# Loading, multiplying and splitting the first gate set of the v stage among the last units of the u stage

## The chip, the cores and the metric

The kernel runs on one core of one Trainium2 chip. The metric is the device time in microseconds (us) of one execution; of several runs the median is given. A separate execution was recorded by the hardware profiler, and its trace is what the rows further down come from.

## The reference, cut to what matters

The reference is a decoder trunk of two layers. Each layer has a mixer, a cross-attention to a memory, and an expert network (PEER); the change touches the expert network alone.

```
def peer_ffn(h, w_pq, sub_keys, expert_u, expert_v):
    q = (h @ w_pq).reshape(B, S, PEER_HEADS, 2, PEER_DQ // 2)
    scores = jnp.einsum('bshpd,hpkd->bshpk', q, sub_keys).astype(jnp.float32)
    top_s, top_i = lax.top_k(scores, K)
...
    best_s, best_pos = lax.top_k(cand_s, K)
    expert_idx = jnp.take_along_axis(cand_i, best_pos, axis=-1)
    gate = jax.nn.softmax(best_s, axis=-1).astype(h.dtype)
...
        u = jnp.take(expert_u, ic, axis=0)
        a = jnp.einsum('cd,chkd->chk', hc, u)
        w = gc * jax.nn.gelu(a, approximate=False)
        return jnp.einsum('chk,chkd->cd', w, jnp.take(expert_v, ic, axis=0))
```

`cand_s` holds the sums of the 16 x 16 pairs of the two halves' best scores. There are 8 heads, 16384 experts, 256 tokens and a model width of 1024. All numbers are float32.

## The kernel before

The kernel does not gather experts. It computes h times the whole of `expert_u` (the **u stage**), takes the Gelu of all of it, multiplies by a dense table of gates that is zero for the experts not chosen, and multiplies the product by the whole of `expert_v` (the **v stage**). Each stage runs over 128 **units**, here u0 to u127 and v0 to v127: a unit is 128 experts, that is one weight tile of 128 x 1024 (512 KB). Both layers run the same code, the second about 1050 us after the first.

**The stream.** All weight tiles of the kernel go through one `Stream` (L26 to L67). Its `load` starts a DMA from SyncE's queue (L49) into one of three `raw` buffers; its `prep` lets ScalarE round the tile to `hi` (L58) and VectorE take the rest `lo` (L60), each into one of three buffers. Before the matmuls of unit n are issued, `get` splits unit n+2 and then starts the load of unit n+5, which waits until the buffer of unit n+2 is split.

**A u unit** (`b_units`, L251 to L254) is 24 matmuls of 256 columns. After every second unit ScalarE and VectorE run `ev_u(i)` for the pair of units 2i and 2i+1: Gelu of the tokens 128 to 255 into `act` (L1005), Gelu of the tokens 0 to 127 into a buffer of the name `tt_` (L1007), which is stored to DRAM as `tdr[i]` while the gates of those tokens are not ready yet, and multiplied into the gate table `gt` (L1013) once they are. `pend` holds an `ev_u` back until the matmuls of the next unit are issued, or until `flush` is called.

**A v unit** (`v_mm`) is 12 matmuls of 512 columns (L1054), whose stationary operand is a split gate set. **Gate set w(n)** serves v(2n) and v(2n+1), and takes two steps. `w_load(n)` starts two DMAs on SyncE's queue into a `tt_` buffer: the gates of the tokens 128 to 255 from the table `gd` in DRAM (L1024), which GpSimd's indirect DMAs have summed up, and `tdr[n]` (L1029). `w_prep(n)` lets VectorE multiply the one half by `act` (L1038) and the other by `gt` (L1040), ScalarE round the set to `oh1` (L1041) and VectorE take the rest to `oh2` (L1042). There are two buffers of each name.

**The order.** Every engine runs its instructions in the order in which this Python code issues them (`manual_schedule`). After u127 the code issues `ev_u(63)`, then `w_load(0)`, `w_load(1)`, `w_prep(0)`, and then, ahead of v0, `w_load(2)` and `w_prep(1)`; ahead of each later even unit v(2n) stand `w_load(n+2)` and `w_prep(n+1)`.

Of the kernel before, what the change touches and what calls it, by code (L numbers as in the profile page):

```python
# [72 lines left out]
def paced(g, rate):  # L73

    credit = 0.0
    while True:
        credit += rate[0]
        while credit > 0:
            c = next(g, g)
            if c is g:  # L80
                return
            if c is None:
                break
            credit -= c
        yield
# [30 lines left out]
def build(tc, ctx, a):  # L116
# [28 lines left out]
    side = Side()  # L145
# [23 lines left out]
    hT = const.tile([128, KT, 512], F32R)  # L169
# [6 lines left out]
    def flush():  # L176
        while pend:
            pend.pop(0)()

    def unit(f):  # L180
        hi, lo = st.get()
        f(hi, lo)
        flush()
        side.tick()
# [55 lines left out]
    def b_units(src, n, evac, first=0):  # L240

        for i in range(first, first + n):
            if i % 2 == 0:
                ps = mm.tile([128, 2, 256], F32, name="mm")

            def f(hi, lo):
                h3 = hi.rearrange("p (k n) -> p k n", k=KT)
                l3 = lo.rearrange("p (k n) -> p k n", k=KT)
                o = ps[:, i % 2]
                for k in range(KT):  # L250
                    T.matmul(o, h3[:, k], src[:, k, 0:256], start=(k == 0), stop=False)  # L251
                    T.matmul(o, h3[:, k], src[:, k, 256:512], start=False, stop=False)  # L252
                for k in range(KT):
                    T.matmul(o, l3[:, k], src[:, k, 0:256], start=False, stop=(k == KT - 1))  # L254
            unit(f)
            if i % 2:
                pend.append(lambda i=i, ps=ps: evac(i // 2, ps))
# [92 lines left out]
    for l in range(L):  # L350
# [628 lines left out]
        direct = []  # L979

        def peer_task():
            for g in range(GROUPS):
                hs = range(HG * g, HG * g + HG)
                yield from keys_of(1, range(2 * hs.start, 2 * hs.stop))
                yield from scattered(hs)
            yield from keys_of(0, range(16))
            yield from select()
            c_top.close()
            gt[0] = pool(c_g1, "gp0").tile([128, 128, 128], F32, name="gt0")
            rate[0] = RATE[1]  # L990
            yield from g_build()
            yield None
            yield None
            direct.append(True)
        rate = [RATE[0]]
        t_p = side.add(paced(peer_task(), rate))
# [7 lines left out]
        def ev_u(i, ps):  # L1004
# [6 lines left out]
            direct.append(i)  # L1011
            g_ = gt[0][:, 2 * i:2 * i + 2]
            V.tensor_mul(g_, g_, t)  # L1013
        b_units(hT, 128, ev_u)
        assert not t_p in side.tasks
        flush()
        i_dir = direct[1]
        tw = {}

        def w_load(n):  # L1020
            if n < 64:
                tw[n] = t = pe.tile([128, 2, 256], F32, name="tt_")
                g_ = gd[l].rearrange("(n c p t) o -> n p c (t o)", c=2, p=128, t=128)
                i_ = nc.sync.dma_start(t[:, :, 128:256], g_[n]).ins  # L1024
                if n == 0:
                    for j_ in late:
                        tc.add_manual_dep(i_, j_.name, SYNC, reason="all gates")
                if n < i_dir:
                    nc.sync.dma_start(t[:, :, 0:128], tdr[n].rearrange("p (c t) -> p c t", c=2))  # L1029

        def w_prep(n):
            if n >= 64:
                return
            wh = pe.tile([128, 2, 256], F32R, name="oh1")
            wl = pe.tile([128, 2, 256], F32R, name="oh2")
            t = tw.pop(n)
            t0, t1 = t[:, :, 0:128], t[:, :, 128:256]
            V.tensor_mul(t1, t1, act[:, 2 * n:2 * n + 2])  # L1038
            if n < i_dir:
                V.tensor_mul(t0, t0, gt[0][:, 2 * n:2 * n + 2])  # L1040
                A.copy(wh, t)  # L1041
                V.tensor_sub(wl, t, wh.bitcast(F32))  # L1042
            else:
                for z, c_ in ((gt[0][:, 2 * n:2 * n + 2], slice(0, 128)), (t1, slice(128, 256))):
                    A.copy(wh[:, :, c_], z)
                    V.tensor_sub(wl[:, :, c_], z, wh[:, :, c_].bitcast(F32))
            tw[n] = (wh, wl)

        def v_mm(i, w, hi, lo, dds=(0, 1), tts=(0, 1)):
            for tt in tts:  # L1050
                h_, l_ = (z[:, i % 2, tt * 128:(tt + 1) * 128] for z in w)
                for st_, mv_, first in ((h_, hi, True), (l_, hi, False), (h_, lo, False)):
                    for dd in dds:
                        T.matmul(out[tt][dd], st_, mv_[:, dd * 512:(dd + 1) * 512],  # L1054
                                 start=(i == 0 and first), stop=(i == 127 and mv_ is lo))
        w_load(0)
        w_load(1)
        w_prep(0)
        c_ps.close()
        ops = pool(c_ps, "ops", space=PS)  # L1060
        out = [[ops.tile([128, 512], F32, name=f"out{tt}{dd}") for dd in range(2)] for tt in range(2)]
        for i in range(126):
            if i % 2 == 0:
                w_load(i // 2 + 2)
                w_prep(i // 2 + 1)
                w = tw.pop(i // 2)
            unit(lambda hi, lo: v_mm(i, w, hi, lo))
# [16 lines left out]
        for dd in range(2):  # L1084
            for tt in range(2):
                for c in range(2):
                    v_mm(126 + c, w, *last[c], (dd,), (tt,))
                if dd and not tt and l + 1 < L:
                    nx.turn(0, False)
                add_x(dd, tt, out[tt][dd])  # L1090
                if l + 1 == L:
                    xg[dd, tt] = new_t()
                    nx.squares(dd, (tt,))
                    V.tensor_mul(xg[dd, tt], x[:, tt, dd * 512:(dd + 1) * 512], gf[dd])
                    if dd:
                        nx.root(slice(tt, tt + 1))
# [92 lines left out]
```

## Time and profile before

| what | value |
|---|---|
| median of 3 runs | 2116.82 us (2116.72 to 2119.5) |
| the profiled execution: its own time | 2121.27 us |
| the profiled execution: its span | 2119.5 us |
| TensorE busy | 2089.5 us, 99% of the span |
| VectorE busy | 1496.0 us, 71% |
| ScalarE busy | 1125.5 us, 53% |
| mean granted TensorE clock | 0.996 |

The span runs from the first to the last instruction of the trace; what lies around it is 1.77 us. A row of the timeline gives the start, the length, the engine, the line and the number of instructions that it merges; behind it in brackets stands how long the engine had been idle, and what ended that. SPq is SyncE's DMA queue, PE is TensorE, DVE VectorE, ACT ScalarE.

### The profile page before, as it was taken

How to read it: one execution, taken by the hardware profiler on the slowest of the kernel's cores; microseconds unless marked ns; L12 is line 12 of the kernel's file. 1: busy time of each engine (PE TensorE's matmuls, PEld its weight loads, DVE VectorE, ACT ScalarE, POOL GpSimd, SP SyncE). 2: the span in 40 equal slices, each digit the busy share in tenths (PEclk: the TensorE clock that was granted, in tenths of full speed). 3: DMA queues.
4: the chain of work that ended last, by engine and by line, in shares of the span. 5: the costliest groups of instructions: out<-in, count | busy, mean ns of one | idle time of the engine just before them, and what ended most of it. 6: DMA issues, size and time to landing. Idle time of an engine off the chain costs nothing.

```text
span 2119.5 us, 35283 instructions
## 1 busy us (share of the span) xinstructions
PE 2089.5 (99%) x13508; PEld 1909.9 (90%) x13508; DVE 1496.0 (71%) x2593; ACT 1125.5 (53%) x1585; POOL 544.4 (26%) x565
## 2 busy tenths in 40 slices
PE   8999999999999999999999999999999999999998
PEld 7899899999999888888888998999999997888886
DVE  5775589988654577776676756999987446777766
ACT  5745556546654444444466455655566544444454
POOL 0120037787820000000012100478877100000000
PEclk9999999999999999999999999999999999999999
DMA  6664458887665677776667545588876656777765
GB/s 240 230 209 161 160 158 206 212 202 178 139 176 180 197 243 240 243 241 218 215 222 251 176 154 172 165 203 217 200 167 147 176 187 203 239 244 239 238 217 174
DMA packets 225609, 426.07 MB, mean 201 GB/s; under 512 B 54304, under 2 KB 134560, under 8 KB 224160
## 3 DMA queue, kind: packets, MB, share of 16 engines
q1 hardware_dynamic: 185696, 415.83, 61.7%
q0 software_dynamic: 36864, 0.15, 4.9%
q10 hardware_dynamic: 2880, 7.85, 1.1%
q8 instruction: 105, 1.72, 0.3%
q14 instruction: 64, 0.52, 0.1%
HBM read 410.50 MB, written 30.02 MB: 208 GB/s over the span
## 4 chain that ended last, share of the span: by engine, by line
PE 68%; issue 23%; POOL 5%; DMA 2%; ACT 1%; DVE 1%; POOLq 0%; SPq 0%; ACTq 0%
PE out L1054 16%; PE mm L252 11%; PE mm L251 11%; PE mm L254 11%; POOL gd L881 5%; PE mm L194 4%; PE mm L196 4%; PE mm L195 4%; PE gps L960 1%; PE sps L807 1%; DMA kt<-keys 1%; PE att L698 1%; PE att L729 1%; DMA gd<-gv,gi 1%; PE att L434 0%
## 5 line engine op out<-in xcount | busy, mean ns | idle before, releaser
L60 DVE TENSOR_TENSOR lo<-raw,hi 128x1024 fp32r<-128x1024 f32 x680 | 831.6, 1228 | 362.3 <-ACT hi L58 355.7
L58 ACT CAST hi<-raw 128x1024 fp32r<-128x1024 f32 x680 | 711.7, 1050 | 465.4 <-PE mm L252 263.1
L251 PE MATMUL mm<-hT,hi 128*128 128x256 f32 x2272 | 563.0, 285 | 0.0
L1054 PE MATMUL out<-hi,oh 128*128 128x512 f32 x2048 | 552.6, 391 | 9.0 <-ACT oh L1041 9.0
L252 PE MATMUL mm<-hT,hi 128*128 128x256 f32 x2272 | 557.1, 283 | 0.0
L881 POOL DMA_INDIRECT gd<-gv,gi x256 | 474.7, 1854 | 199.7 <-DVE tv L794 81.3
L1054 PEld LDWEIGHTS out<-hi,oh 128*128 128x128 f32 x2048 | 386.6, 189 | 90.0 <-ACT oh L1041 9.4
L251 PEld LDWEIGHTS mm<-hT,hi 128*128 128x128 f32 x2272 | 436.1, 192 | 0.3
L252 PEld LDWEIGHTS mm<-hT,hi 128*128 128x128 f32 x2272 | 435.7, 192 | 0.2
L254 PE MATMUL mm<-hT,lo 128*128 128x256 f32 x2272 | 318.8, 283 | 0.0
L1054 PE MATMUL out<-lo,oh 128*128 128x512 f32 x1024 | 317.8, 390 | 0.0
L260 POOL TENSOR_TENSOR rstd<-rstd,mhalf 128x2 f32<-128x2 f32 (+1 forms) x8 | 5.5, 688 | 1180.4 <-DVE rstd L300 1180.4
L254 PEld LDWEIGHTS mm<-hT,lo 128*128 128x128 f32 x2272 | 293.0, 192 | 0.0
L1054 PEld LDWEIGHTS out<-lo,oh 128*128 128x128 f32 x1024 | 193.1, 189 | 40.4
L889 POOL MEMSET mhalf<- 1x1 f32 x256 | 159.1, 622 | 0.0
L961 ACT ACTIVATE gt<-gps 128x512 f32<-128x512 f32 x64 | 68.9, 1114 | 40.4 <-PE gps L960 40.4
L966 DVE TENSOR_TENSOR oh<-slot 128x1024 f16<-128x1024 f16 x64 | 44.2, 690 | 51.3 <-PE gps L960 51.2
L960 PE MATMUL gps<-oh,oh 128*128 128x128 f16 x512 | 68.7, 296 | 0.4 <-issue 0.2
L194 PE MATMUL mm<-hi,hT 128*128 128x512 f32 x160 | 64.0, 400 | 0.0
L196 PE MATMUL mm<-lo,hT 128*128 128x512 f32 x160 | 62.6, 391 | 0.0
L195 PE MATMUL mm<-hi,hT 128*128 128x512 f32 x160 | 62.4, 390 | 0.0
L960 PEld LDWEIGHTS <-oh 128*128 128x128 f16 x512 | 53.9, 118 | 3.6 <-issue 0.8
(911 smaller groups left out, 2345.7 us busy)
## 6 DMA issues: line engine op xcount, KB each, us to landing
raw<-u SPq DMA_DIRECT2D x256, 512.0 KB
raw<-v SPq DMA_DIRECT2D x256, 512.0 KB
raw<-w_in_a SPq DMA_DIRECT2D x40, 512.0 KB
gd<-zeros SPq DMA_DIRECT2D x64, 256.0 KB
raw<-pq SPq DMA_DIRECT2D x32, 512.0 KB
raw<-w_in_b SPq DMA_DIRECT2D x16, 512.0 KB
raw<-wkv_b SPq DMA_DIRECT2D x16, 512.0 KB
raw<-w_out SPq DMA_DIRECT2D x16, 512.0 KB
```

The costliest lines, as they stand in the source:

```text
L58: self.nc.scalar.copy(hi, r)
L60: self.nc.vector.tensor_sub(lo, r, hi.bitcast(F32))
L194: T.matmul(ps[tt], sh, h3[:, kk], start=(k == 0), stop=False)
L195: T.matmul(ps[tt], sl, h3[:, kk], start=False, stop=False)
L196: T.matmul(ps[tt], sh, l3[:, kk], start=False, stop=(k == KT - 1))
L251: T.matmul(o, h3[:, k], src[:, k, 0:256], start=(k == 0), stop=False)
L252: T.matmul(o, h3[:, k], src[:, k, 256:512], start=False, stop=False)
L254: T.matmul(o, l3[:, k], src[:, k, 0:256], start=False, stop=(k == KT - 1))
L881: i_ = G.indirect_dma_start(gd[l], bass.IndirectOffsetOnAxis(ap=gi[:, h, c:c + 1], axis=0), gv[:, h, c:c + 1], None, compute_op=OP.add).ins
L889: G.memset(mhalf[0:1, 8:9], 0.0)
L960: T.matmul(ps[:, i], a0[:, 1, :, i], b0[:, w, :, i], start=(w == 0), stop=(w == 1))
L1054: T.matmul(out[tt][dd], st_, mv_[:, dd * 512:(dd + 1) * 512], start=(i == 0 and first), stop=(i == 127 and mv_ is lo))
```

## The change

`w_load(0)` is issued after u123 in place of after u127, and `w_prep(0)` after u125. For this `flush` is called after u123 too, so that `ev_u(61)` is issued ahead of the split of u126 in place of behind the matmuls of u124. `w_load(1)` stays behind `ev_u(63)`, and all that follows stays as it was. The definitions of `w_load`, `w_prep` and `v_mm` move up in the text, unchanged but that `i_dir` is now written `direct[1]`. No instruction is added or taken away. L1024, L1029, L1038, L1040, L1041, L1042 and L1054 of before are L1020, L1025, L1034, L1036, L1037, L1038 and L1050 of the changed kernel.

```
-        b_units(hT, 128, ev_u)
-        assert not t_p in side.tasks
-        flush()
-        i_dir = direct[1]
         tw = {}
...
-                if n < i_dir:
+                if n < direct[1]:
...
+        b_units(hT, 124, ev_u)
+        flush()
+        assert not t_p in side.tasks
         w_load(0)
+        b_units(hT, 2, ev_u, 124)
+        w_prep(0)
+        b_units(hT, 2, ev_u, 126)
+        flush()
         w_load(1)
-        w_prep(0)
         c_ps.close()
```

**SyncE's queue at the end of the u stage, layer 0.** The five tiles `raw` are those of v0 to v4; `tt__8435` is the buffer of w(0) before and `tt__8305` that of after, the next ones are w(1) and w(2). Before:

```order
L49 DMA raw_8275<-v 128x1024
L49 DMA raw_8306<-v 128x1024
L49 DMA raw_8340<-v 128x1024
L49 DMA raw_8371<-v 128x1024
L49 DMA raw_8405<-v 128x1024
L1024 DMA tt__8435<-gd0_94 128x2x128
L1029 DMA tt__8435<-tdr_96 128x2x128
L1024 DMA tt__8438<-gd0_94 128x2x128
L1029 DMA tt__8438<-tdr_96 128x2x128
L1024 DMA tt__8456<-gd0_94 128x2x128
```

After:

```order
L49 DMA raw_8275<-v 128x1024
L1020 DMA tt__8305<-gd0_94 128x2x128
L1025 DMA tt__8305<-tdr_96 128x2x128
L49 DMA raw_8313<-v 128x1024
L49 DMA raw_8343<-v 128x1024
L49 DMA raw_8380<-v 128x1024
L49 DMA raw_8414<-v 128x1024
L1020 DMA tt__8444<-gd0_94 128x2x128
L1025 DMA tt__8444<-tdr_96 128x2x128
L1020 DMA tt__8456<-gd0_94 128x2x128
```

The two loads of w(0) have moved from behind the tile of v4 to behind the tile of v0, and the loads of w(1) now stand where those of w(0) stood.

**ScalarE at the end of the u stage, layer 0.** The first `hi` of each list is that of u126, the next ones are u127, v0, v1 and v2; the pairs L1005 and L1007 are `ev_u(61)`, `ev_u(62)` and `ev_u(63)`. Before:

```order
L58 CAST hi_8302<-raw_8210 128x1024
L1005 ACTIVATE act_3204<-mm_8236 128x256
L1007 ACTIVATE tt__8333<-mm_8236 128x2x128
L58 CAST hi_8336<-raw_8241 128x1024
L58 CAST hi_8367<-raw_8275 128x1024
L1005 ACTIVATE act_3204<-mm_8301 128x256
L1007 ACTIVATE tt__8398<-mm_8301 128x2x128
L58 CAST hi_8401<-raw_8306 128x1024
L1005 ACTIVATE act_3204<-mm_8366 128x256
L1007 ACTIVATE tt__8432<-mm_8366 128x2x128
L1041 CAST oh1_8441<-tt__8435 128x512
L1041 CAST oh1_8459<-tt__8438 128x512
```

After:

```order
L1005 ACTIVATE act_3204<-mm_8236 128x256
L1007 ACTIVATE tt__8302<-mm_8236 128x2x128
L58 CAST hi_8309<-raw_8210 128x1024
L58 CAST hi_8339<-raw_8241 128x1024
L1037 CAST oh1_8369<-tt__8305 128x512
L58 CAST hi_8376<-raw_8275 128x1024
L1005 ACTIVATE act_3204<-mm_8308 128x256
L1007 ACTIVATE tt__8407<-mm_8308 128x2x128
L58 CAST hi_8410<-raw_8313 128x1024
L1005 ACTIVATE act_3204<-mm_8375 128x256
L1007 ACTIVATE tt__8441<-mm_8375 128x2x128
L1037 CAST oh1_8459<-tt__8444 128x512
```

The rounding of w(0) has moved from behind `ev_u(63)` to ahead of the split of v0, `ev_u(61)` has moved ahead of the split of u126, and the rounding of w(1) still stands behind `ev_u(63)` and ahead of the split of v2. VectorE's list moves in the same way. The order of TensorE's matmuls is unchanged.

## Rows read from the trace of the kernel before

**Rows 1.** Part 1 of the page: busy time of each engine.

```profile
PE 2089.5 (99%) x13508; PEld 1909.9 (90%) x13508; DVE 1496.0 (71%) x2593; ACT 1125.5 (53%) x1585; POOL 544.4 (26%) x565
```

**Rows 2.** Waits of TensorE: in total (us), times, longest; the two largest.

```profile
PE out L1054 <- ACT oh L1041: 9.0, 2, 4.8
PE mm L267 <- DMA cm<-c_main: 3.8, 1, 3.8
```

**Rows 3.** Timeline of TensorE, layer 0: end of u127, start of v0, v1.

```profile
705.14 1.12 PE L254 MATMUL mm<-hT,lo 128*128 128x256 f32 x8
...
711.02 2.07 PE L1054 MATMUL out<-hi,oh 128*128 128x512 f32 x4 [4.76 <-ACT oh L1041]
...
715.75 1.07 PE L1054 MATMUL out<-hi,oh 128*128 128x512 f32 x4
```

**Rows 4.** The same in layer 1; the last row is the 19th matmul.

```profile
1754.92 1.12 PE L254 MATMUL mm<-hT,lo 128*128 128x256 f32 x8
...
1760.27 2.07 PE L1054 MATMUL out<-hi,oh 128*128 128x512 f32 x4 [4.22 <-ACT oh L1041]
...
1767.33 1.08 PE L1054 MATMUL out<-hi,oh 128*128 128x512 f32 x4
```

**Rows 5.** Windows: length, busy time per engine, granted clock, DMA share, GB/s.

```profile
259.00:260.00 1.00, 0.27 (x3) 0.08 (x2) 0.10 (x1) 0.00 (x0) 0.00 (x0) 1.00 0.67 250
260.00:261.00 1.00, 0.99 (x8) 1.00 (x9) 0.00 (x0) 0.22 (x1) 0.00 (x0) 1.00 1.03 307
...
711.02:715.30 4.28, 4.28 (x10) 3.32 (x11) 3.26 (x5) 1.57 (x2) 0.00 (x0) 0.52 0.21 61
1760.27:1766.87 6.60, 6.60 (x17) 5.11 (x17) 4.07 (x6) 2.61 (x3) 0.00 (x0) 0.54 0.27 94
718.00:1048.00 330.00, 330.00 (x1457) 273.26 (x1456) 231.50 (x304) 161.18 (x200) 0.00 (x0) 1.00 0.76 234
```

**Rows 6.** Timeline of w(0) from its loads to its rounding, both layers.

```profile
705.42 0.39 SPq L1024 DMA_DIRECT2D tt__8435<-gd  x1
705.86 0.59 SPq L1029 DMA_DIRECT2D tt__8435<-tdr  x1
...
709.52 0.42 DVE L1038 TENSOR_TENSOR tt__8435<-tt__8435,act 128x256 f32<-128x256 f32 x1 [2.11 <-DMA tt__8435<-gd]
709.89 0.43 DVE L1040 TENSOR_TENSOR tt__8435<-tt__8435,gt 128x256 f32<-128x256 f32 x1
710.35 0.62 ACT L1041 CAST oh<-tt__8435 128x512 fp32r<-128x512 f32 x1 [3.40 <-DVE tt__8435 L1040]
...
1755.20 0.48 SPq L1024 DMA_DIRECT2D tt__19653<-gd  x1
...
1758.60 0.42 DVE L1038 TENSOR_TENSOR tt__19653<-tt__19653,act 128x256 f32<-128x256 f32 x1 [1.40 <-DMA tt__19653<-gd]
1759.14 0.42 DVE L1040 TENSOR_TENSOR tt__19653<-tt__19653,gt 128x256 f32<-128x256 f32 x1
1759.60 0.62 ACT L1041 CAST oh<-tt__19653 128x512 fp32r<-128x512 f32 x1 [2.86 <-DVE tt__19653 L1040]
```

**Rows 7.** Timeline, layer 0: tile loads, splits of u127, v0; w(1)'s rounding, split of v2.

```profile
693.27 11.85 SPq L49 DMA_DIRECT2D raw<-v  x5
...
697.78 1.23 DVE L60 TENSOR_TENSOR lo<-raw,hi 128x1024 fp32r<-128x1024 f32 x1 [1.32 <-ACT hi L58]
...
699.58 1.05 ACT L58 CAST hi<-raw 128x1024 fp32r<-128x1024 f32 x1 [1.83 <-PE mm L252]
...
712.40 0.62 ACT L1041 CAST oh<-tt__8438 128x512 fp32r<-128x512 f32 x1 [1.43 <-DVE tt__8438 L1040]
712.92 1.04 ACT L58 CAST hi<-raw 128x1024 fp32r<-128x1024 f32 x1
...
714.00 1.22 DVE L60 TENSOR_TENSOR lo<-raw,hi 128x1024 fp32r<-128x1024 f32 x1 [0.26 <-ACT hi L58]
```

**Rows 8.** Timeline of TensorE: a short wait earlier in layer 0.

```profile
260.01 0.68 PE L807 MATMUL sps<-kt,q 128*128 128x128 f32 x4 [0.75 <-DMA kt<-keys]
```

More of the change, by code (lines that the diff above doesn't have):

```diff
@@ L1038, in w_prep @@
             V.tensor_mul(t1, t1, act[:, 2 * n:2 * n + 2])
-            if n < i_dir:
+            if n < direct[1]:
                 V.tensor_mul(t0, t0, gt[0][:, 2 * n:2 * n + 2])
```

## The prediction

> **What bounds the kernel now.** I read the page's busy times first: TensorE is busy for 2089.5 of 2119.5 us [rows 1], so the time is TensorE's own work plus what little it stands idle, and 30 us is all that any reordering could touch. The waits of TensorE come next, to see where that idle time sits: the largest entry is 9.0 us in two waits, both of the first matmul of the v stage, for ScalarE's rounding of a gate set [rows 2]. That is one wait in each layer, at just the place that the change moves. The timeline of both places then says what one such wait costs, and here there is more than the idle time.
>
> Layer 0. The eight last matmuls of u127 start at 705.14, and eight of 0.28 us that fill 1.12 start 0.12 apart; so the next matmul would be due at 705.14 + 8 x 0.12 = 706.10. It starts at 711.02 [rows 3]: 4.92 us lost. In the long middle of the v stage 1457 matmuls take 330 us, 0.2265 each, at a granted clock of 1.00 [rows 5]. The 13th matmul of the stage would so be due 12 x 0.2265 = 2.72 after the first, at 713.74, and starts at 715.75 [rows 3]: another 2.01 us lost, in a stretch in which the granted clock was 0.52, that is the lower of the two levels (1.2 GHz) nearly throughout [rows 5]. Before the clock fell, TensorE had done nothing but wait.
>
> Layer 1 reads the same: due at 1754.92 + 0.96 = 1755.88, started at 1760.27, 4.39 lost; the 19th matmul due 18 x 0.2265 = 4.08 later at 1764.35, started at 1767.33 [rows 4], 2.98 lost at a granted clock of 0.54 [rows 5].
>
> The two places cost 4.92 + 2.01 + 4.39 + 2.98 = **14.30 us**. Of this 9.31 is waiting and 4.99 is the clock.
>
> **Why TensorE waits there.** SyncE starts the loads of w(0) at 705.42, when the u stage is all but over; the first multiplication starts 4.10 later, the rounding 0.83 after that at 710.35, and TensorE 0.67 after that [rows 6, 3]. In layer 1 the load takes 3.40 [rows 6]. Nothing in this chain needs the end of the u stage; it is only issued there.
>
> **The change, part by part.**
>
> *The loads of w(0)* now stand behind the tile load of v0, which starts at 693.27 [rows 7], so they start at about 693.7 (the gates themselves were summed long before). By the two loads of before they are there 3.4 to 4.1 later, by 697.8. Queued behind them on SyncE are the tile loads of v1 to v4; each of these waits for a split that comes later anyway, the first at some 697, and the two loads hold SyncE for 0.39 + 0.59 us [rows 6]. Cost nothing.
>
> *The early flush* puts `ev_u(61)` ahead of the split of u126 on ScalarE and VectorE. That split comes some 1.6 us later by the length of what is now ahead of it; u126 starts on TensorE at 706.10 - 2 x 2.88 = 700.34, over 2 us after the split is done. Cost nothing, and u127's split waits for TensorE as before.
>
> *The multiplications and the split of w(0)* follow VectorE's part of u127, which runs from 697.78 for 1.23 [rows 7]. So they start at 699.0, and with the steps of before (0.37, 0.46, and a rounding of 0.62 [rows 6]) the rounding runs from 699.85 to 700.45. Queued behind it on ScalarE is the rounding of v0's tile, which ran at 699.58 [rows 7] and now starts at some 700.4; with 1.08 until VectorE starts on its part and 1.22 for that (712.92, 714.00 [rows 7]) v0 is split at 702.7. TensorE needs it at 706.10: a cover of 3.4 us. If the load of w(0) came late, the first 1.2 us (697.8 to 699.0) and then these 3.4 would have to go before TensorE waits. So v0 starts at 706.10 and 1755.88, all 9.31 us of waiting go, and as nothing is left that idles TensorE, the 4.99 of the clock go too.
>
> *What is late next: w(1).* Its loads take exactly the place on SyncE that those of w(0) had, behind the tile of v4, and its rounding stands ahead of v2's split on ScalarE. So I take w(1) at the times that w(0) had: rounding at 710.35, v2's rounding 0.52 later (712.40 to 712.92 [rows 7]) from 710.87 to 711.92, VectorE's part from 711.95 to 713.17. But v2 is now due at 706.10 + 24 x 0.2265 = 711.54. It waits 0.38 for `hi`, and its fifth matmul, the first that uses `lo`, is due at 711.92 + 0.91 = 712.83 and waits another 0.34. In layer 1 the rounding at 1759.60 [rows 6] gives `hi` at 1761.17 against 1761.32, no wait, and `lo` at 1762.42 against 1762.23: 0.19. Together 0.38 + 0.34 + 0.19 = **0.91 us** given back. From both sides: nothing, if the loads of w(1) land some 0.7 earlier than those of w(0) did; or about 3 us a layer if they land 2.5 later. I take 0.91, since the loads before them in the queue are the same.
>
> The Trainium skill, DMA: Bandwidth & Descriptors, section Anatomy of one DMA, gives a DMA some 2.0 us and then its bytes at 436 GB/s; for 128 KB that is an estimate of 2.3 us. The rows here say 3.4 and 4.1, with other transfers under way, and the measurement decides; by the page v2 would not wait at all and the sum would be 14.3.
>
> *After v2.* Each later set has the same buffers and the same order as before. From 718 to 1048 TensorE never idled [rows 5], with VectorE busy for 231.5 of 330 us and ScalarE for 161.2, so the split has room to catch up; a set that is 0.4 late at v2 is not late again at v6.
>
> **The sum.** 14.30 - 0.91 = 13.39 us. Span: 2119.5 - 13.4 = 2106.1, and the profiled execution's own 2121.27 would be 2107.9. That execution was 4.45 us above the median of the runs; I take the same 13.4 off the median: 2116.82 - 13.4 = **2103.4 us**.
>
> **The rivals.**
>
> *The clock is not given back.* The new short waits at v2 could make the clock fall as the long ones did, or the timed runs could lose less to the clock than the profiled one. Then only 9.31 - 0.91 = 8.4 go: 2108.4. Against it: a wait of 0.75 us earlier in the layer [rows 8] left the granted clock at 1.00 in the windows around it [rows 5], and the waits that I expect are shorter. The Trainium skill, TensorE: Matmul & The Clock Gate, section A second HAM failure mode, tells of short idles between groups of matmuls that made the clock go back and forth; one or two waits do not repeat like that, and the trace speaks against it. Chance 0.08.
>
> *The wait moves to w(1) and grows (slower than before).* Before, a late w(1) was covered by the 7 us of layer 0's gap and slow clock; now nothing covers it. Each us that its loads land later is one us at v2, and a wait that long would bring the slow clock back at 2.0 to 3.0 a layer. A layer breaks even at a wait of about 7.15 - 2.5 = 4.65 us, a landing some 4 us later than rows 6 show, at 8 us in place of 4.1. At 12 us in both layers it would be 2 x (8.4 + 2.5) = 21.8 against 14.3 saved: 2124.3. For it: more data is now asked for in less time. Against it: the DMAs stood at a share of 0.76 at full pace [rows 5], and no load in rows 6 took over 4.1. Chance 0.05.
>
> *The change does nothing.* The order on SyncE, ScalarE and VectorE does move; but if the load of w(0) took over 10 us from 693.7, for instance behind the tile loads, TensorE would wait as before: 2116.8. Chance 0.04.
>
> **How the numbers follow.** About 0.2%, 4.2 us here, is what a measurement of this kernel can tell from no change. Forecast with its own bounds (up to 3 us more wait, up to 1 us less): 0.83, faster. Clock not given back: 0.08, faster. Slower rival: 0.05, of which all is slower. No change: 0.04. So faster 0.91, same 0.04, slower 0.05. Range: the low end has the clock cost 2.98 in both layers and no new wait, 2116.82 - (9.31 + 5.96) = 2101.5; the high end is the first rival's, 2108.4. Between them lies over 0.8.
>
> **What would show it.** In the profile of the changed kernel: no wait of TensorE before the first v matmul; a granted clock of 1.00 in the 5 us after it; the first gate multiplication near 699.0 and the next one near 709.5; a wait of TensorE of at most 0.4 us at v2, for `hi` or `lo`; a span near 2106. It would be wrong if the first v matmul still waits, if v2 waits for over 1 us, or if the clock falls in its first units.

## The result and the profile after

The changed kernel takes 2106.51 us (median of 4 runs, 2105.09 to 2109.22), the kernel before 2117.68 us (2116.72 to 2119.5). The ratio is 0.9948 with a 95% interval of 0.9931 to 0.9965: 11.2 us by the medians, 11.0 (7.4 to 14.6) by the ratio. The forecast was 13.4 us, a time of 2103.4. One timed execution of the kernel without the early flush (e5 below) ran at a mean granted clock of 0.851 and took 2259.15 us; it is left out of e5's median and ratio.

The profiled execution of the changed kernel has a span of 2107.4 us. The waits of TensorE answer to [rows 2]: in total, times, longest.

```profile
PE mm L267 <- DMA cm<-c_main: 4.0, 1, 4.0
PE mm L228 <- ACT hi L58: 1.9, 1, 1.9
PE att L434 <- issue: 1.5, 1, 1.5
PE out L1050 <- ACT hi L58: 1.2, 1, 1.2
```

The two waits for the rounding of w(0), 9.0 us, are gone. One wait of a v matmul is left, 1.2 us, and it is for the `hi` of a tile. The timeline of TensorE in layer 0, which answers to [rows 3], says which tile:

```profile
702.96 1.12 PE L254 MATMUL mm<-hT,lo 128*128 128x256 f32 x8
703.92 1.09 PE L1050 MATMUL out<-hi,oh 128*128 128x512 f32 x4
...
708.93 0.61 PE L1050 MATMUL out<-lo,oh 128*128 128x512 f32 x2
710.73 1.20 PE L1050 MATMUL out<-hi,oh 128*128 128x512 f32 x4 [1.18 <-ACT hi L58]
711.99 0.73 PE L1050 MATMUL out<-lo,oh 128*128 128x512 f32 x2
712.56 1.08 PE L1050 MATMUL out<-hi,oh 128*128 128x512 f32 x4
713.48 0.62 PE L1050 MATMUL out<-lo,oh 128*128 128x512 f32 x2
713.93 1.07 PE L1050 MATMUL out<-hi,oh 128*128 128x512 f32 x4
```

v0 is due at 702.96 + 8 x 0.12 = 703.92 and starts at 703.92. The 25th matmul, the first of v2, is due 24 x 0.2266 = 5.44 later at 709.36 and starts at 710.73: 1.37 lost. The 37th, the first of v3, is due at 712.08 and starts at 713.93: 1.85 lost by then. Of the further 0.48 us, 0.36 lie ahead of the first `lo` matmul of v2, which starts 1.26 behind the first of v2 where 0.91 is the usual distance, and 0.12 right behind it. In layer 1, which answers to [rows 4], the same reading gives:

```profile
1749.39 1.12 PE L254 MATMUL mm<-hT,lo 128*128 128x256 f32 x8
1750.36 1.09 PE L1050 MATMUL out<-hi,oh 128*128 128x512 f32 x4
...
1756.13 1.20 PE L1050 MATMUL out<-hi,oh 128*128 128x512 f32 x4
1757.39 0.74 PE L1050 MATMUL out<-lo,oh 128*128 128x512 f32 x2
...
1759.36 1.08 PE L1050 MATMUL out<-hi,oh 128*128 128x512 f32 x4
```

v0 starts at its due time; v2 is 0.34 late, v3 0.85, and 0.87 stays lost. The windows, columns as in [rows 5], show the clock around the wait at v2 in both layers:

```profile
706.00:711.00 5.00, 3.82 (x17) 2.89 (x16) 1.75 (x4) 1.89 (x3) 0.00 (x0) 1.00 0.26 78
711.00:712.00 1.00, 0.94 (x5) 0.41 (x4) 1.00 (x2) 0.62 (x1) 0.00 (x0) 1.00 0.00 0
...
1755.00:1760.00 5.00, 4.79 (x20) 3.31 (x19) 3.84 (x6) 2.79 (x5) 0.00 (x0) 1.00 0.31 103
```

The granted clock is 1.00 in all of them, through the wait of 1.18 us too. So the two places lose 1.85 + 0.87 = 2.72 us where they lost 14.30: 11.58 us gained at the places that the change touches, against 11.2 by the medians. The spans differ by 12.1. The other 0.5 us is the balance of two differences in stretches in which the change moves nothing: the u stage of layer 0 ended 2.18 earlier (703.92 against 706.10), and from v3 of layer 0 to v0 of layer 1 the execution took 1.73 longer; among the waits in between, that of L434 is the largest.

The rows of w(0) and w(1) answer to [rows 6]; here are those of layer 0, then the loads and first multiplication of w(1) in layer 1.

```profile
691.72 0.39 SPq L1020 DMA_DIRECT2D tt__8305<-gd  x1
...
703.04 0.43 SPq L1020 DMA_DIRECT2D tt__8444<-gd  x1
...
696.74 0.42 DVE L1034 TENSOR_TENSOR tt__8305<-tt__8305,act 128x256 f32<-128x256 f32 x1
...
708.31 0.43 DVE L1034 TENSOR_TENSOR tt__8444<-tt__8444,act 128x256 f32<-128x256 f32 x1 [3.08 <-DMA tt__8444<-gd]
...
709.11 0.62 ACT L1037 CAST oh<-tt__8444 128x512 fp32r<-128x512 f32 x1 [4.33 <-DVE tt__8444 L1036]
709.63 1.99 ACT L58 CAST hi<-raw 128x1024 fp32r<-128x1024 f32 x2
...
1749.47 1.42 SPq L1020 DMA_DIRECT2D tt__19662<-gd  x1
...
1753.46 0.43 DVE L1034 TENSOR_TENSOR tt__19662<-tt__19662,act 128x256 f32<-128x256 f32 x1 [1.79 <-DMA tt__19662<-gd]
```

w(0) is loaded 12.2 us ahead of v0's due time and multiplied 7.2 ahead of it, without a wait. w(1) is what TensorE now waits for, by way of v2's tile: its load takes 5.27 us from its issue to the first multiplication (3.99 in layer 1), the rounding follows 0.80 later, and v2's rounding is queued behind that.

### The profile page after: what moved, and what is told of

Read it like the earlier page. It is cut to its first block, busy times and chain, and to the rows that moved or that the text cites. A ratio compares the mean times of both kernels' runs of the same rounds, so it can differ in the third digit from the quotient of the medians.

```text
span 2107.4 us, 35289 instructions
## 1 busy us (share of the span) xinstructions
PE 2085.3 (99%) x13508; PEld 1906.2 (90%) x13508; DVE 1494.4 (71%) x2593; ACT 1124.7 (53%) x1585; POOL 541.0 (26%) x565
## 4 chain that ended last, share of the span: by engine, by line
PE 66%; issue 24%; POOL 5%; DMA 2%; DVE 2%; ACT 1%; SPq 0%; POOLq 0%; ACTq 0%; DVEq 0%
PE out L1050 16%; PE mm L252 11%; PE mm L251 11%; PE mm L254 11%; POOL gd L881 5%; PE mm L194 4%; PE mm L196 4%; PE mm L195 4%; PE gps L960 1%; PE sps L807 1%; PE att L698 1%; PE att L729 1%; DVE lo L60 1%; DMA gd<-gv,gi 1%; ACT hi L58 0%
## 5 line engine op out<-in xcount | busy, mean ns | idle before, releaser
L1050 PE MATMUL out<-hi,oh 128*128 128x512 f32 x2048 | 549.1, 389 | 1.3 <-ACT hi L58 1.2
L1050 PEld LDWEIGHTS out<-hi,oh 128*128 128x128 f32 x2048 | 384.1, 188 | 81.9 <-ACT hi L58 2.2
L1050 PE MATMUL out<-lo,oh 128*128 128x512 f32 x1024 | 316.7, 389 | 0.1
L1050 PEld LDWEIGHTS out<-lo,oh 128*128 128x128 f32 x1024 | 192.1, 188 | 40.6 <-DVE lo L60 1.0
```

## The experiments

For each kernel the table gives how late v0 starts and what is lost in all by v5 (the 61st matmul), worked out as above from the timeline of its profiled execution, and the time. Beside each median stands that of the kernel before, measured with it on the same chip.

| kernel | layer 0: v0, v5 | layer 1: v0, v5 | lost in both | median us (before) | ratio, 95% interval |
|---|---|---|---|---|---|
| before | 4.92, 6.93 | 4.39, 7.38 | 14.3 | | |
| changed | 0, 1.85 | 0, 0.87 | 2.7 | 2106.51 (2117.68) | 0.9948 (0.9931 to 0.9965) |
| changed, a1 | 0, 1.50 | 0, 0.61 | 2.1 | 2108.19 (2118.67) | 0.9954 (0.9941 to 0.9968) |
| changed, a2 | 0, 1.20 | 0, 0.53 | 1.7 | 2107.22 (2118.51) | 0.9944 (0.9930 to 0.9958) |
| e1, gap filled | 4.23, 4.64 | 4.37, 4.79 | 9.4 | 2114.41 (2118.67) | 0.9978 (0.9969 to 0.9988) |
| e2, loads alone | 2.68, 3.13 | 2.68, 4.66 | 7.8 | 2113.92 (2118.67) | 0.9978 (0.9967 to 0.9988) |
| e3, w(1) loaded early | 0, 0.03 | 0, 0.03 | 0.1 | 2105.11 (2118.67) | 0.9937 (0.9924 to 0.9951) |
| e4, v2 split first | 0, 0.03 | 0, 0.83 | 0.9 | 2106.04 (2118.35) | 0.9945 (0.9932 to 0.9959) |
| e5, no early flush | 0, 0.41 | 0, 0.62 | 1.0 | 2108.25 (2118.35) | 0.9957 (0.9942 to 0.9971) |
| e7, the same again | 0, 1.76 | 0, 0.79 | 2.6 | 2108.39 (2118.51) | 0.9949 (0.9935 to 0.9963) |
| e6, 1 MB ahead of w(1) | 0, 5.72 | 0, 6.54 | 12.3 | 2116.74 (2118.35) | 0.9994 (0.9984 to 1.0003) |
| e6, 2 MB ahead of w(1) | 0, 8.99 | 0, 8.58 | 17.6 | 2122.72 (2118.35) | 1.0029 (1.0018 to 1.0040) |

**The gap with TensorE at work.** Is the slow start of the v stage a price of the idle time, or would the first v matmuls be slow anyway? The kernel before, with filler:

```
         w_load(0)
         w_load(1)
         w_prep(0)
+        fill = mm.tile([128, 2, 256], F32, name="mm")
+        for k in range(32):
+            T.matmul(fill[:, 0], hT[:, k % KT, 0:128], hT[:, k % KT, 0:256], start=(k == 0), stop=(k == 31))
```

> The kernel before, with 32 matmuls of 256 columns into a spare accumulator issued between u127 and v0, so that TensorE works through most of the gap while w(0) is fetched and split as before. Their result is not used. They take 32 x 0.12 = 3.8 us of a gap of 4.2 to 4.8. Theory (a gap costs its idle time and then a stretch at the lower clock): v0 starts as late as before, 4.9 and 4.4 us behind its due time, but the granted clock stays at 1.00, the 13th matmul of layer 0 and the 19th of layer 1 come 2.0 and 3.0 us earlier against the first, and the time falls by 5.0 us. Rival (the first matmuls of the v stage are slow for another reason, such as new weights or accumulators): the clock or the spacing is as before, no change in time.

Measured: 4.3 us faster by the medians, 4.7 (2.5 to 6.6) by the ratio. The timeline of TensorE in layer 0, and two windows:

```profile
705.10 4.00 PE L1061 MATMUL mm<-hT 128*128 128x256 f32 x32
709.33 1.46 PE L1054 MATMUL out<-hi,oh 128*128 128x512 f32 x4 [0.22 <-ACT oh L1041]
710.62 0.62 PE L1054 MATMUL out<-lo,oh 128*128 128x512 f32 x2
...
712.46 1.07 PE L1054 MATMUL out<-hi,oh 128*128 128x512 f32 x4
...
705.00:709.30 4.30, 4.10 (x35) 3.90 (x33) 1.19 (x3) 1.28 (x3) 0.00 (x0) 1.00 0.72 231
709.30:714.00 4.70, 4.67 (x19) 3.58 (x20) 3.75 (x6) 2.60 (x3) 0.00 (x0) 1.00 0.19 56
```

v0 still starts 4.2 us late, for w(0), but the clock stays at 1.00 and the 13th matmul comes 3.13 after the first where it came 4.73 after it before [rows 3]. The timed executions say the same: all ten of this kernel have a mean granted clock of 0.999, the nineteen of the kernel before beside it 0.995 to 0.998. So the slow clock is the price of the idle gap. The price is a little less than the forecast said: 0.41 and 0.42 us are lost behind v0 even so, nearly all by its fifth matmul; two of the first four need the remainder of w(0) (`oh2`), which VectorE starts on only as v0 starts. At the slow clock that wait was hidden. Of the 4.99 us behind v0, filling the gap gives back 4.2 and leaves 0.83 as this wait; with w(0) early both go.

**The loads alone.** Which part of the change does the work?

```
         b_units(hT, 2, ev_u, 124)
-        w_prep(0)
         b_units(hT, 2, ev_u, 126)
         flush()
         w_load(1)
+        w_prep(0)
```

> The changed kernel with the multiplications and the split of w(0) put back behind ev_u(63); only its loads stay early. Theory: VectorE starts on w(0) when ev_u(63) is done, 1.3 us after v0 is due, and v0 starts 2.75 us late in each layer; v2 does not wait, since it is due 2.75 later too. If so short a gap leaves the clock at 1.00, 2 x 2.75 = 5.5 us are lost of the 14.3 lost before: 8.8 faster than before, near 2108.9. Rival (a gap of over 2 us brings the lower clock too): 2 x 2.5 more, 3.8 faster than before, near 2113.9.

Measured: 4.7 us faster by the ratio (2.5 to 7.0), 4.8 by the medians, nearer to the 3.8 of the rival than to the 8.8 of the theory. v0 starts 2.68 late in both layers, where 2.75 was expected, and v2 does not wait. In layer 0 of the profiled execution the clock stays at 1.00. In layer 1 it does not, after the same gap; the first row is v0 in layer 0, then come the windows around v0 in layer 1 for TensorE alone (length, its busy time and instructions, granted clock, DMA share, GB/s), and the timeline there:

```profile
709.89 1.47 PE L1050 MATMUL out<-hi,oh 128*128 128x512 f32 x4 [2.53 <-ACT oh L1037]
...
1755.00:1755.62 0.62, 0.00 (x0) 1.00 0.24 85
1755.62:1756.20 0.58, 0.58 (x2) 1.00 0.60 178
1756.20:1756.80 0.60, 0.60 (x2) 0.57 0.76 225
1756.80:1757.40 0.60, 0.60 (x3) 0.50 0.04 13
...
1755.62 1.95 PE L1050 MATMUL out<-hi,oh 128*128 128x512 f32 x4 [2.53 <-ACT oh L1037]
1757.37 1.05 PE L1050 MATMUL out<-lo,oh 128*128 128x512 f32 x2
1758.22 1.77 PE L1050 MATMUL out<-hi,oh 128*128 128x512 f32 x4
1759.83 0.63 PE L1050 MATMUL out<-lo,oh 128*128 128x512 f32 x2
```

So neither side is right alone: a gap of 2.53 us costs the clock at one place and not at the other. The two losses sum to 7.8 us, 6.5 less than before; the medians say 4.8. The traced execution has a mean granted clock of 0.999 and the seven others 0.997 to 0.998, which fits a clock that falls in both layers there; but the traced one was also the slowest of the eight (2115.73), so how often the clock falls is not shown. The loads alone give about half of the change (4.8 of 10.5 us by the medians beside each other, 6.5 of 12.2 by the traces); the split of w(0) among the last units gives the rest.

**The loads of w(1) early.** The changed kernel with

```
+        pend.append(lambda: w_load(1))
         b_units(hT, 2, ev_u, 126)
         flush()
-        w_load(1)
```

> The changed kernel with the loads of w(1) issued right behind ev_u(62), so that they stand ahead of the tile load of v4 on SyncE. Theory (what the forecast lost against the result is the wait at v2, which is set by when w(1) lands): the loads start about 3.2 us before v0 is due instead of 0.9 and land before ev_u(63) is done; v2 is split by 6.0 us after v0's due time and does not wait; the 1.85 and 0.84 us lost in v2 and v3 go, 2.7 us faster than the changed kernel. Rival (the wait at v2 is set by the order on ScalarE or by v2's tile): the same time as the changed kernel.

and the changed kernel beside it:

> The changed kernel once more, beside the others on one chip. Theory: no wait ahead of v0, clock at 1.00, a wait at v2 whose length follows the landing of w(1) (3.99 to 5.27 us after its issue in the first profile): between 0.2 and 2 us in each layer; 10 to 13 us faster than before.

Measured: 2105.11 us (2103.54 to 2106.86) against 2108.19 (2106.98 to 2109.74), five runs each: 3.1 us faster, where 2.7 were expected. In layer 0, SyncE, VectorE, and TensorE at v2:

```profile
701.04 0.43 SPq L1020 DMA_DIRECT2D tt__8410<-gd  x1
...
705.43 0.42 DVE L1034 TENSOR_TENSOR tt__8410<-tt__8410,act 128x256 f32<-128x256 f32 x1
...
709.21 0.62 PE L1050 MATMUL out<-lo,oh 128*128 128x512 f32 x2
709.66 1.07 PE L1050 MATMUL out<-hi,oh 128*128 128x512 f32 x4
710.57 0.62 PE L1050 MATMUL out<-lo,oh 128*128 128x512 f32 x2
```

The load starts 3.15 ahead of v0 (704.19), the first multiplication waits for nothing but VectorE, and v2 starts 0.45 behind the matmul before it like any other. In layer 1 the load takes 4.98 us and the first multiplication waits 0.51 for it, but v2 does not wait. Both places now lose 0.03 us. By its ratio this kernel is 13.3 us (10.4 to 16.1) faster than the one before, of 14.3 that could be had. It beats the kernel before clearly; against the changed kernel beside it every execution is faster, while the intervals of the two ratios overlap.

**The split of v2 ahead of w(1).** How much of the wait at v2 is the landing, and how much the order on ScalarE?

```
             if i % 2 == 0:
                 w_load(i // 2 + 2)
-                w_prep(i // 2 + 1)
+                if i:
+                    w_prep(i // 2 + 1)
                 w = tw.pop(i // 2)
             unit(lambda hi, lo: v_mm(i, w, hi, lo))
+            if not i:
+                w_prep(1)
```

> The changed kernel with w_prep(1) issued behind v0's matmuls in place of ahead of them, so that the split of v2's tile stands ahead of the rounding of w(1) on ScalarE and VectorE. The loads stay where they are. Theory (the wait at v2 is the landing of w(1) plus the split of v2's tile that is queued behind it): the landing stays, the 1.6 us of the split behind it go; what v0 to v2 lose against their due time falls from 1.5 to 1.9 us to under 0.8 in layer 0 and from 0.6 to 0.8 us to nothing in layer 1, some 1.9 us faster than the changed kernel and about 1 us slower than with w(1) loaded early. Rival (only the landing counts): as the changed kernel.

Measured: 0.9 us lost, 2106.04 us. In layer 0 w(1) was first multiplied 4.30 after its issue and v2 did not wait. In layer 1, where no loss was expected, it took 5.24, the longest there, and v2 did:

```profile
1751.57 0.42 DVE L1034 TENSOR_TENSOR tt__19662<-tt__19662,act 128x256 f32<-128x256 f32 x1 [1.30 <-DMA tt__19662<-gd]
...
1752.36 0.62 ACT L1037 CAST oh<-tt__19662 128x512 fp32r<-128x512 f32 x1 [3.35 <-DVE tt__19662 L1036]
...
1753.03 1.47 PE L1050 MATMUL out<-hi,oh 128*128 128x512 f32 x4 [0.19 <-ACT oh L1037]
```

v2 waits for w(1) itself here, 1.46 after its first multiplication; in the changed kernel it is 2.42 (708.31 to 710.73). So about 1 us of the way to v2 is the order on ScalarE, less than the 1.6 expected, since the set's own rounding and start remain. In time the kernel can't be told from the changed one (0.9945 against 0.9944 to 0.9954).

**No early flush.**

```
         b_units(hT, 124, ev_u)
-        flush()
         assert not t_p in side.tasks
```

> The changed kernel without the early flush: ev_u(61) stays behind the matmuls of u124, as before the change. Theory (the flush costs nothing, its delay is covered): the split of u126 comes 1.6 us earlier, TensorE does not notice, v2 waits as in the changed kernel (1.5 to 1.9 us lost in layer 0, 0.6 to 0.8 in layer 1), the time is the same within 1 us. Rival (the later splits push the tile loads of v1 and v3 into the loads of w(1)): w(1) lands up to 1 us earlier in each layer and up to 2 us go.

Its first profile lost 0.41 us in layer 0, less than any of the changed kernel, so it ran once more beside the changed kernel:

> The kernel without the early flush once more, beside the changed kernel on one chip. In its first profile v0 to v2 lost 0.41 and 0.62 us where the changed kernel lost 1.85 and 0.87, and 1.50 and 0.61. Theory (the flush costs nothing, the landing of w(1) varies by up to 1 us from run to run): the time is within 1 us of the changed kernel, and the losses of this run overlap with those of the changed kernel. Rival (the flush makes w(1) land later in layer 0): again under 0.8 in layer 0, some 1.2 us faster than the changed kernel.

> The changed kernel a third time, for the run before it in this list. Theory: 0.4 to 1.9 us lost in layer 0, 0.4 to 0.9 in layer 1. Rival: 1.5 or more in layer 0 again.

The second time it lost 1.76 and 0.79, and took 2108.39 us against 2107.22. That is 1.2 us more, where at most 1 was expected; the losses overlap. The rival falls: the flush has no cost that these runs can tell, and the landing of w(1) varies. From issue to first multiplication it took 5.27, 4.92 and 4.62 us in layer 0 of the changed kernel, 3.86 and 5.23 without the flush; in layer 1 3.99, 4.01, 3.95, 4.04 and 4.24.

**w(1) held up.** The changed kernel with 2 or 4 more transfers of 512 KB ahead of w(1):

```
     tdr = dram.tile([64, 128, 256], F32)
+    spare = dram.tile([L, 4, 128, 1024], F32)
...
         flush()
+        for k in range(2):
+            nc.sync.dma_start(spare[l, k], a["v"][l, k])
         w_load(1)
```

> The changed kernel with two more transfers of 512 KB each (tiles of expert_v copied to a spare place in DRAM, not used) ahead of the loads of w(1) on SyncE, in each layer. Theory of the slower rival (each us that w(1) lands later is a us at v2): at the 330 to 385 GB/s that the busiest us of the profiles show, 1 MB holds w(1) up by some 3 us; v2 waits 4 to 5 us in layer 0 and 3 to 4 in layer 1, and the granted clock falls in at least one layer. 6 to 11 us slower than the changed kernel, at most as slow as before. Against it (the transfers run beside each other or v2 has slack): under 3 us slower.

> The same with four more transfers of 512 KB. Theory: w(1) lands some 6 us later, v2 waits 7 to 8 us in each layer and the granted clock falls in both; 2 x (6 + 2.5) = 17 us slower than the changed kernel and so slower than the kernel before by some 6 us. Against it: not slower than the kernel before.

Measured: with 1 MB 1.6 us under the kernel before beside it, from which it can't be told by the ratio; the changed kernel was 10.5 to 11.3 under in its three measurements, so this is some 9 us slower. With 2 MB 4.4 us above the kernel before (6.1, 3.8 to 8.5, by the ratio). v2 waited 3.47 and 4.64 us with 1 MB, in the other order of the layers than expected, and 6.05 and 6.78 with 2 MB, a little less than expected. Waits of TensorE with 1 MB, then layer 0 of both:

```profile
PE out L1051 <- ACT hi L58: 8.1, 2, 4.6
...
713.91 1.20 PE L1051 MATMUL out<-hi,oh 128*128 128x512 f32 x4 [3.47 <-ACT hi L58]
715.17 1.09 PE L1051 MATMUL out<-lo,oh 128*128 128x512 f32 x2
716.06 1.91 PE L1051 MATMUL out<-hi,oh 128*128 128x512 f32 x4
...
714.88 2.08 PE L1051 MATMUL out<-hi,oh 128*128 128x512 f32 x4 [6.05 <-ACT hi L58]
```

The wait at v2 follows the landing, and in all four places the slow clock comes with it (1.91 for four matmuls in place of 1.07). The slower rival is a real mechanism. At about the time of the kernel before, w(1) was first multiplied 6.7 and 7.9 us behind the start of v0 (1 MB); the break-even of the forecast, 8 us from an issue 0.7 ahead of v0, comes to 7.3. The latest without added transfers is 4.4.

## Why the prediction was right

**The two gaps.** Both went in full: v0 starts at its due time in both layers, in every traced execution that has the whole of w(0) early. The forecast had the load start about 12.4 us and the first multiplication 7.1 us ahead of v0; they came out at 12.2 and 7.2. How long the load took can't be read, since nothing waited for it; it was there within the 5.0 us to the first multiplication, so the rival by which the change does nothing falls too.

**The clock.** The 4.99 us went too, though e1 shows that 0.83 of them would have stayed, as a wait for the remainder of w(0) that the slow clock had covered. The term was right and its name was partly wrong: it went in full because the early split brings the remainder early as well. The 30 us of idle time are thus not all that a reordering can touch: matmuls at the slow clock count as busy, and TensorE's busy time fell from 2089.5 to 2085.3 us, with e3 to 2082.8.

**The new wait at v2: the step that was mis-sized.** The forecast took w(1) at the times that w(0) had, 4.10 and 3.40 us from issue to first multiplication, and so had 0.91 us given back. It was 2.72, and 2.1 and 1.7 in the two repeats, since the loads took 4.6 to 5.3 in layer 0 and 4.0 in layer 1; against v0's due time the first multiplication came up to 0.97 later in layer 0 and 0.4 in layer 1. Put into the working of the forecast, the later multiplications alone make its 0.72 and 0.19 us some 1.7 and 0.6, of 1.85 and 0.87 measured, so the mechanism was right and the landing was mis-sized. A load that was measured twice was given one value each, when its spread was the size of the term. The forecast's own sign of being wrong, a wait of over 1 us at v2, was met in the first profile (1.18) and not in the two repeats (0.8 and 0.5). The bound on the other side, no wait at all if the loads land early enough, is what e3 brought about, and with it the sum of 14.3.

Why the loads of w(1) take longer than those of w(0) did is not shown. The later loads of the tiles ahead are not the cause: e5 and e7 are one kernel and took 3.86 and 5.23. What the rows do show is that the loads before them in the queue are the same, but not as far ahead. In the changed kernel the issue of w(1) follows that of v4's tile within 0.05 us, where that of w(0) stood 0.3 behind it before; in e2, where it stands 2.3 behind it, w(1) was multiplied 2.52 and 2.71 us after its issue. No run varies this distance alone. In layer 0 of e2:

```profile
698.76 7.46 SPq L49 DMA_DIRECT2D raw<-v  x4
708.54 0.38 SPq L1020 DMA_DIRECT2D tt__8438<-gd  x1
...
711.06 0.42 DVE L1034 TENSOR_TENSOR tt__8438<-tt__8438,act 128x256 f32<-128x256 f32 x1 [0.49 <-DMA tt__8438<-gd]
```

**The time.** The median is 3.1 us above the forecast. Of this 1.8 are the wait at v2 and 0.9 the kernel before, whose median rose from 2116.82 to 2117.68 with one more execution; the 0.4 left are less than the runs of one kernel differ by.

**The estimate from the Trainium skill.** DMA: Bandwidth & Descriptors, section Anatomy of one DMA, gives its 2.0 us and 436 GB/s for DMAs that GpSimd issues; these loads go by SyncE's queue. The estimate of 2.3 us that the forecast works out from it was further off than the forecast: in the changed kernel no load of w(1) came under 3.95, right behind a tile of 512 KB. Only in e2, 2.3 us behind that tile, were they near it (2.52 and 2.71). The measurements decide.

**The rivals.** The clock was given back: a wait of 1.18 us at v2 left it at 1.00. The wait at v2 did grow, but stayed far from the break-even of 4.65 us a layer; e6 brackets that number, with waits of 3.5 and 4.6 at about the time of before and 6.1 and 6.8 above it.

**What else.** The early flush has no cost that e5 and e7 can tell, as worked out. After v2 nothing more is lost in the changed kernel: what is lost at v3 is lost at v5 to within 0.02, and the rest of the stage shows no wait.

## What to carry to other kernels

Where a stage begins with a load, a multiplication and a split that depend on nothing the stage before still computes, issue all of it, the split too, a few units earlier: the loads alone gave about half. Then do the same for the second set at once, since it takes over the place of the first; ask when it lands against when it is needed, and give that landing its spread, not one value. Price an idle gap of the matmul engine by where its matmuls stand after the clock is back, not by the idle time: here 9.3 us of waiting cost 14.3.

## What the runs showed of the hardware that was not expected

The granted clock can fall after TensorE has gone back to work. In e2, layer 1, it was 1.00 at the end of a wait of 2.53 us and in the first two matmuls, and fell to 0.50 between 0.6 and 1.2 us after they began; in e6 with 1 MB the first four matmuls after 3.47 us ran at full pace and the next at half. The same 2.53 us in layer 0 of e2 cost no clock. So whether a gap of 2.5 us is paid for with the clock differs from place to place. The waits of 0.75 us [rows 8], 1.18 us and 1.77 us (e2, L807 in layer 0) were not paid for, and all six of 3.47 us and more ahead of a v matmul were. The Trainium skill, TensorE: Matmul & The Clock Gate, section What's actually happening, has the gate set by how busy the array has been of late; a fall behind the gap agrees with that.

At the very start of the kernel the granted clock of the rows does not fit the pace of the matmuls. In the changed kernel it reads 1.00 in the first 16 us, but the matmuls of 256 columns between 8.94 and 10.23 us start 0.21 us apart, and only from 17.2 us on 0.12. So the waits there, of up to 4 us, say nothing on the price of a gap; the readings at the v stage hold, because there the spacing of the matmuls and the granted clock agree.
